# Last phase of a streaming encoder layer: transposes of u and y by the transfer engines, cached keys through two PSUM banks

## The chip, the cores and the metric

The kernel runs on one core of a Trainium2 chip. A core has five instruction streams that matter here: TensorE (PE, with its weight loads PEld), VectorE (DVE), ScalarE (ACT), GpSimd (POOL) and SyncE (SP); the last does nothing but issue transfers, which 16 DMA engines carry out. Every stream runs its instructions in the order in which they stand in it. The metric is the time of one execution in microseconds of device time. Before the change it is 2327.88 us, the median of three runs between 2325.01 and 2328.12.

## The reference

One layer of an encoder with two token mixers that work side by side, on a prompt of 2048 rows (16 tiles of 128) and on a "sample" batch of 8 sequences of 16 rows (one more tile of 128 rows), each sequence with 512 cached keys and values. Cut to what matters:

```
h, gate = adaln_modulate(x, c, norm_g, w_ada, b_ada)
qa, ka, va, za, qb, kb, vb, zb, ga, gb = project_inputs(h, w_in, pos)
oa = diff_attention(qa, ka, va, qpos, kpos, lam)          # 4 heads, two softmaxes each
ob = stick_breaking_attention(qb, kb, vb, qpos, kpos)     # 8 heads
oa = rms_norm(oa, subln_g) * (1.0 - lam_init)
ya = (oa.reshape(b, s, WIDTH_A) * silu(za)) @ w_branch_a  # 512 -> 1024
yb = (ob.reshape(b, s, WIDTH_B) * silu(zb)) @ w_branch_b  # 512 -> 1024
y  = sigmoid(ga) * ya + sigmoid(gb) * yb
x  = x + gate * (y @ w_out)                               # 1024 -> 1024
out = rms_norm(x, final_g)
```

For the sample rows the keys and values are the cached ones with the new ones behind them. The keys and values of all rows are outputs too.

## The kernel before

Up to about 1780 us of the profile the kernel projects h and runs the prompt's attention, one head (or pair of heads) after another, called a unit (8 units). z, the gates g, the attention's output o and, for the sample rows, q, k and v go to DRAM. The attention weights of the prompt are transposed there by transposing transfers (`turn`, line 568), which SP issues: for each, up to 128 rows by 2048 numbers of two bytes become 16 blocks of 128 x 128. These transfers are the one part of the kernel before that does with another tile what the change does with u and y.

The **last phase** (from line 1294 on, with its first tile begun earlier) goes through the 17 tiles of 128 rows, the sample tile as the last but one. For each tile:

- `inputs` (line 1162) loads o (line 1165) and z (line 1166), both into one buffer each (hs[0], hs[1]), and two halves of the gates (line 1170) into one of two pairs of buffers; it forms u = norm(o) * silu(z), and writes it as two float16 numbers, high and low part, into `u16` (hs[2], one buffer for all tiles).
- `turned` (line 1195) transposes u16, 16 blocks of 128 x 128: `transposed` (line 1155) sends 8 blocks through TensorE (line 1159) into one PSUM bank, and ScalarE copies the bank to SBUF (line 1160); twice. The destination has two buffers.
- `branches` (line 1201) multiplies u with the two branch weights: 48 matmuls of 512 columns (line 1210), four results of 12. VectorE and GpSimd apply the gates (lines 1212 and 1214), and `finish` splits the sum y into `y16`, high and low (lines 287 and 292), one buffer for all tiles.
- `turned_y` (line 1233) transposes y16 in the same way; here the destination has one buffer too, so the transpose of a tile's y waits until the products of the tile before have read theirs.
- `output` (line 1331) multiplies y with w_out: 48 matmuls of 512 columns (line 1344), two results of 24, then adds x, normalizes and stores (line 1358). The x of a tile is loaded at line 1337.

The sample attention runs beside the tiles. Eight units go through steps: four loads of keys (tile `dk`, line 716, two buffers) and four of values (`dv`, four buffers), 512 KB each; the transposes of the cached keys (line 735: two halves per load, four blocks each, into one PSUM bank `t` of which there is one, evicted to `dks` by VectorE for the first half and by ScalarE for the second, line 736); queries (line 721); scores (lines 745, 746, 752); weights (line 770, which waits for the softmax or the products on VectorE and GpSimd) and values (lines 784, 788).

In the source the work of step n is an interleaving, by written costs, of the branches of tile n, the output of tile n-1 and some steps of the sample units. The final order is set by a scheduler that plays the program through with its own costs of each instruction and lets each stream take what it takes to be ready; a change of one instruction's cost can therefore move many others. PSUM has eight banks: `mm` 2, `s` 3, `t` 1, `o` 2.

Of the kernel before, what the change touches and what calls it, by code (L numbers as in the profile page):

```python
# [17 lines left out]
F16 = mybir.dt.float16  # L18
# [7 lines left out]
P = 128  # L26
D = 1024
KT = D // P
# [82 lines left out]
def layer_kernel(ctx: ExitStack, tc: tile.TileContext, a: dict):  # L111
    nc = tc.nc
    V, S, G, T = nc.vector, nc.scalar, nc.gpsimd, nc.tensor
# [73 lines left out]
    def bank(tag, dt=F32):  # L187
        return ps.tile([P, 512 if dt == F32 else 1024], dt, tag=tag, name=f"ps_{tag}", bufs=BANKS[tag])
# [4 lines left out]
    id16 = con.tile([P, P], F16, name="id16")  # L193
# [507 lines left out]
    def sample(U, dec, fixed):  # L701
# [28 lines left out]
        def keys(i, half):  # L730
            if half == 0:
                box["k", i] = dec.tile([P, 8, P], F32, tag="dks", name="dks", bufs=4)
            pt = bank("t")
            for j in range(4):
                T.transpose(pt[:, j * P : (j + 1) * P], box[nk, i][:, half * 4 + j, :], ident)
            (S.copy if half else V.tensor_copy)(out=box["k", i][:, half * 4 : half * 4 + 4, :], in_=pt.rearrange("p (j n) -> p j n", n=P))
# [65 lines left out]
        for i in range(4):  # L802
            steps[2 + i] += [one(keys, i, 0), one(keys, i, 1)]
# [90 lines left out]
    with tc.tile_pool(name="p0", bufs=1) as p0:  # L894
# [25 lines left out]
        pt = bank("t")  # L920
# [231 lines left out]
        split(dst[:, 0, :, :], dst[:, 1, :, :], st, s, S if n % 2 else G)  # L1152
        return dst

    def transposed(x16, dst, half):

        pt = bank("s", F16)
        for k in range(KT):
            T.transpose(pt[:, k * P : (k + 1) * P], x16[:, half, k * P : (k + 1) * P], id16)  # L1159
        S.copy(out=dst[:, half * KT : (half + 1) * KT, :], in_=pt.rearrange("p (k n) -> p k n", n=P))  # L1160

    def inputs(t):

        o, z = hs[0:2]
        load(out=o, in_=o_d[t])
        load(out=z, in_=z_d[t])
        gs = []
        for j in range(2):
            gs.append(L["g"][(2 * len(begun) + j) % 4].rearrange("p (b n) -> p b n", b=2))
            load(out=gs[j], in_=g_d[t].rearrange("p (b n) -> p b n", b=2)[:, :, j * 512 : (j + 1) * 512])  # L1170
        begun.append(t)
        r = L["orms"][:, 4 * t : 4 * t + 4] if t < NT else rsqrt(osums[:, NT, :], 4, P, tiny, "rA")
        for n in range(2):
            c = slice(n * 512, (n + 1) * 512)
            sg = bank("mm")
            act(out=sg, in_=z[:, c], func=AF.Sigmoid)
            G.tensor_tensor(out=o[:, c], in0=o[:, c], in1=z[:, c], op=ALU.mult)
            if n == 1:
                V.tensor_tensor(out=o[:, c], in0=o[:, c], in1=sg, op=ALU.mult)  # L1179
            else:  # L1180
                for h in range(4):
                    c = slice(h * P, (h + 1) * P)
                    V.scalar_tensor_tensor(out=o[:, c], in0=sg[:, c], scalar=r[:, h : h + 1], in1=o[:, c], op0=ALU.mult, op1=ALU.mult)  # L1183
        for g in gs:
            act(out=g, in_=g, func=AF.Sigmoid)
        acc = tiny.tile([P, 1], F32, tag="uacc", name="uacc")
        sum_squares(o, D, acc)
        su = scales(acc, unit, "su")
        u16 = hs[2].bitcast(F16).rearrange("p (f n) -> p f n", f=2)
        split(u16[:, 0, :], u16[:, 1, :], o, su[:, 0:1], S)  # L1190
        iu = unit.tile([P, 1], F32, tag="iu", name="iu")
        V.tensor_tensor(out=iu, in0=su[:, 1:2], in1=L["s"][0][:, 1:2], op=ALU.mult)
        return dict(u16=u16, u=L["u"][len(begun) % 2], iu=iu, g=gs)

    def turned(st):

        st["u"] = st["u"].bitcast(F16).rearrange("p (k n) -> p k n", n=P)
        for half in range(2):
            transposed(st["u16"], st["u"], half)

    def branches(st):

# [29 lines left out]

    def turned_y(st):
        st["y"] = yT = L["y"].bitcast(F16).rearrange("p (k n) -> p k n", n=P)
        for half in range(2):
            transposed(st["y16"], yT, half)


    tiles = list(range(NT - 1)) + [NT, NT - 1]
# [15 lines left out]
    def early_work():  # L1255


        free.extend(units[7]["bufs"])

        def first(t):  # L1260
            if "orms" not in L:
                L["orms"] = rsqrt(osums[:, 0:NT, :].rearrange("p t h -> p (t h)"), 4 * NT, P, con, "orms")
            states[t] = inputs(t)
            if t == tiles[0]:
                turned(states[t])

        def early(i):

            if i == 0:
                L["first"] = [fn for _, fn in branches(states[tiles[0]])] + [lambda: turned_y(states[tiles[0]])]  # L1270
            L["first"][i]()

        def rest():
            L["g"], L["u"], (L["y"], L["y16"]) = free[0:4], free[4:6], free[6:8]

        return [branch_weight for _ in branch_weights] + [rest] + [lambda t=t: first(t) for t in tiles[0:2]] \
            + [lambda i=i: early(i) for i in range(5)]

    for n in range(first_step, len(steps) + PV_LAG):
        if n < len(steps):  # L1280
            u, t = steps[n]
# [23 lines left out]
    with ExitStack() as c2:  # L1305
# [8 lines left out]
        for j in range(2):  # L1314
            for k in range(0, KT, 2):
                st = s2.tile([P, D], F32, tag="x", name="x", bufs=2)
# [67 lines left out]
        for n in range(NT + 2):  # L1384
            work = []
            if 0 < n <= NT:
                work += branches(states[tiles[n]])
            if n + 1 <= NT:

                work.insert(2, (0.9, lambda n=n: turned(states[tiles[n + 1]])))  # L1390
            if n + 2 <= NT:
                work.insert(5, (0.1, lambda n=n: states.update({tiles[n + 2]: inputs(tiles[n + 2])})))
            if n > 0:
                work += output(tiles[n - 1], states.pop(tiles[n - 1]))
            if 0 < n <= NT:
                work.append((0.9, lambda n=n: turned_y(states[tiles[n]])))
            interleave(work, aside(n))
# [27 lines left out]
```

## Time and profile before

| | |
|---|---|
| median of three runs | 2327.88 us |
| the profiled execution: its own time | 2324.14 us |
| its span, first to last instruction | 2322.4 us |
| granted TensorE clock, mean | 0.971 |
| PE busy | 2115.7 us (91%) |
| DVE, ACT, POOL busy | 1615.7, 1545.4, 686.8 us |
| share of the 16 DMA engines of queue q1 | 67.0% |

The profile is of one execution. "Busy" adds up the time in which an engine has an instruction in work; TensorE's instructions overlap at their ends, so a short group of matmuls shows a few tenths of a microsecond more than its share of the stream. "Idle before" an instruction is the time for which its engine had nothing in work, with what ended it. A row of a timeline gives start, length, engine, line, operation, written tile <- read tiles, and the number of instructions merged into it. The DMA share is the mean busy share of 16 engines; packets overlap, so it can pass 1 for short times.

### The profile page before, as it was taken

The page shows a single profiled execution, that of the slowest core. Times are in us where ns is not written, and L with a number is a line of the kernel's source. Part 1 is how long each engine was busy: PE and PEld are TensorE (multiplying, and loading weights), DVE is VectorE, ACT ScalarE, POOL GpSimd, SP SyncE. Part 2 cuts the span into 40 slices and gives each one's busy share as a digit, 9 for nine tenths or more (in the row PEclk, how much of TensorE's full clock was granted, in tenths as well). Part 3 has the DMA queues.
Part 4 walks back from the last instruction along what each step waited for, and adds up shares of the span by engine and source line. Part 5 has one row for each costly group of instructions (what it writes and reads, how often), then busy time and mean ns, then how long its engine had stood idle before and what let it go on. Part 6 is the DMA issues. An engine that isn't in the chain of part 4 may idle for free. (4 is left out here: it accounts for less than half of the span.)

```text
span 2322.4 us, 41702 instructions
## 1 busy us (share of the span) xinstructions
PE 2115.7 (91%) x15022; PEld 1144.7 (49%) x15022; DVE 1615.7 (70%) x3523; ACT 1545.4 (67%) x3036; POOL 686.8 (30%) x575
## 2 busy tenths in 40 slices
PE   4997998998999999899999989999977889989898
PEld 2544554554555455455545545555544444545443
DVE  4677866789876678978667898776787545564654
ACT  3876767788766677876767787666776545465552
POOL 1522012255301235530123553022345222221222
PEclk8998999999999999999999999999978999999999
DMA  8559669697765679775576876667686766565521
GB/s 291 207 138 258 168 136 219 152 212 165 203 150 127 154 152 206 178 172 134 125 165 153 207 175 168 144 142 163 150 188 177 226 191 184 179 186 150 157 100 56
DMA packets 693840, 395.23 MB, mean 170 GB/s; under 512 B 454810, under 2 KB 638410, under 8 KB 693120
## 3 DMA queue, kind: packets, MB, share of 16 engines
q1 hardware_dynamic: 692554, 392.08, 67.0%
q8 instruction: 118, 1.93, 0.3%
q14 instruction: 90, 0.74, 0.1%
q10 hardware_dynamic: 1078, 0.48, 0.1%
HBM read 212.58 MB, written 72.91 MB: 123 GB/s over the span
## 5 line engine op out<-in xcount | busy, mean ns | idle before, releaser
L613 POOL TENSOR_TENSOR sc_p<-sc_p,sc_n 128x127 f32<-128x127 f32 (+7 forms) x192 | 308.3, 1610 | 782.1 <-DVE sc_n L607 761.7
L423 PE MATMUL ps_mm<-wb,hs 128*128 128x512 f16 x1632 | 412.2, 383 | 5.4 <-ACT gt L498 5.4
L423 PEld LDWEIGHTS <-hs 128*128 128x128 f16 x2976 | 263.1, 99 | 253.5 <-issue 21.2
L423 PE MATMUL ps_mm<-wa,hs 128*128 128x512 f16 x1344 | 337.0, 382 | 6.5 <-DVE v L292 4.7
L607 DVE TENSOR_TENSOR_SCAN sc_n<-ps_s,sc_n,zero_t 128x512 f32<-128x512 f32 x192 | 245.4, 1278 | 76.8 <-ACT ps_s L120 74.8
L120 ACT ACTIVATE sc_p<-ps_s,usc 128x512 f32<-128x512 f32 (+3 forms) x320 | 201.9, 631 | 99.7 <-PE ps_s L631 61.0
L630 PE MATMUL ps_s<-k,qst 128*128 128x512 f16 (+3 forms) x640 | 224.9, 352 | 42.6 <-DVE sc_n L607 31.7
L562 DVE TENSOR_TENSOR sc_n<-sc_p,sc_n 128x128 f16<-128x128 f32 (+7 forms) x192 | 211.6, 1108 | 44.3 <-ACT sc_n L561 44.1
L631 PE MATMUL ps_s<-k,qst 128*128 128x512 f16 (+3 forms) x640 | 224.9, 352 | 0.0
L682 PE MATMUL ps_o<-v,wt 128*128 128x128 f16 x1088 | 192.3, 225 | 28.3 <-DMA wt<-sc_n 28.2
L495 PE MATMUL ps_mm<-wa,hs 128*128 128x512 f16 x816 | 203.3, 379 | 1.2 <-DVE wa L292 1.2
L495 PE MATMUL ps_mm<-wb,hs 128*128 128x512 f16 x816 | 203.2, 379 | 0.0
L495 PEld LDWEIGHTS <-hs 128*128 128x128 f16 x1632 | 140.5, 98 | 123.3 <-issue 1.4
L561 ACT CAST sc_n<-sc_p 128x128 f16<-128x128 f32 (+7 forms) x192 | 153.0, 802 | 61.1 <-POOL sc_p L613 60.9
L120 ACT ACTIVATE ps_s<-ps_s,usc 128x512 f32<-128x512 f32 (+3 forms) x320 | 193.4, 604 | 0.0
L1344 PE MATMUL ps_o<-wo,wb 128*128 128x512 f16 x816 | 187.2, 382 | 0.7 <-ACT wb L1160 0.7
L683 PE MATMUL ps_o<-v,wt 128*128 128x64 f16 x1088 | 173.9, 198 | 0.0
L682 PEld LDWEIGHTS <-wt 128*128 128x128 f16 x1088 | 107.3, 101 | 107.5 <-DMA wt<-sc_n 35.4
L457 POOL TENSOR_TENSOR rot<-pr,rope 128x256 f32<-128x256 f32 x68 | 64.2, 944 | 272.7 <-ACT pr L437 224.7
L683 PEld LDWEIGHTS <-wt 128*128 128x128 f16 x1088 | 105.2, 100 | 72.2 <-issue 1.9
L607 DVE TENSOR_TENSOR_SCAN sc_n<-ps_s,zero_t 128x128 f32<-128x128 f32 (+3 forms) x128 | 104.6, 818 | 49.4 <-ACT ps_s L120 47.6
L1210 PE MATMUL ps_mm<-wa,wb 128*128 128x512 f16 x510 | 125.7, 385 | 3.1 <-DVE hs L1179 1.1
(327 smaller groups left out, 4290.8 us busy)
## 6 DMA issues: line engine op xcount, KB each, us to landing
hs<-hT_d SPq DMA_DIRECT2D x124, 512.0 KB, 4.2
g_d<-gt SPq DMA_DIRECT2D x68, 256.0 KB, 3.7
out_dram<-pr SPq DMA_DIRECT2D x204, 64.0 KB, 2.0
wide<-in_w_ada_dram SPq DMA_DIRECT2D x12, 1024.0 KB, 11.5
wa<-in_w_in_dram SPq DMA_DIRECT2D x36, 256.0 KB, 5.5
z_d<-pr SPq DMA_DIRECT2D x136, 64.0 KB, 1.7
o_d<-o SPq DMA_DIRECT2D x136, 64.0 KB, 2.5
hs<-z_d SPq DMA_DIRECT2D x17, 512.0 KB, 4.6
```

The source lines that it names most:

```text
L120: i = S.activation(**kw)
L423: T.matmul(box["p"], box["h"][:, hi, k, :], U["w"][k][:, wi, :], start=(n == 0), stop=(n == 3 * KT - 1))
L495: T.matmul(box["g"][:, 0:gw], box["h"][:, hi, k, :], U["wg"][k // per][:, k % per, wi, :], start=(j == 0), stop=(j == 3 * KT - 1))
L561: S.copy(out=hi, in_=src)
L562: V.tensor_tensor(out=lo, in0=src, in1=hi, op=ALU.subtract)
L607: V.tensor_tensor_scan(out=dst[:, lo : lo + n][:, ::-1], data0=src[:, 0:n][:, ::-1], data1=zero_t[:, 0:1].to_broadcast([P, n]), initial=fi ...
L613: G.tensor_tensor(out=p[:, 0:m], in0=p[:, 0:m], in1=n[:, 1 : m + 1], op=ALU.mult)
L630: T.matmul(p[:, 0:n], qst[:, c, :], kk[:, c, 0:n], start=True, stop=False)
L631: T.matmul(p[:, 0:n], qst[:, 2 + c, :], kk[:, c, 0:n], start=False, stop=not diag)
L682: T.matmul(po[:, c * P : (c + 1) * P], wt[:, wj, :], vt[:, c, :, :], start=first, stop=False)
L683: T.matmul(po[:, c * P : c * P + 64], wt[:, nb + wj, :], vt[:, c, 0, :], start=False, stop=last)
L1344: T.matmul(po, st["y"][:, yi * 8 + k, :], wo[j * 4 + k // 2][:, wi, k % 2, :], start=(n == 0), stop=(n == 3 * KT - 1))
```

## The change

Two edits, both in the last phase.

1. `turned` and `turned_y` no longer use TensorE and ScalarE. Each issues one transposing transfer on SP: 128 rows of 2048 float16 numbers become 16 blocks, u16 to the tile of u and y16 to the tile of y. The function `transposed` is gone, and with it per tile 32 transposes on TensorE, 4 copies on ScalarE and 4 uses of the PSUM banks `s`.
2. The two halves of a load of cached keys are transposed into different PSUM banks: the first half into `t` as before, the second into one of the three `s`.

```
@@ keys
-            pt = bank("t")
+            pt = bank("ts"[half])
             for j in range(4):
                 T.transpose(pt[:, j * P : (j + 1) * P], box[nk, i][:, half * 4 + j, :], ident)
             (S.copy if half else V.tensor_copy)(out=box["k", i][:, half * 4 : half * 4 + 4, :], in_=pt.rearrange("p (j n) -> p j n", n=P))
@@
-    def transposed(x16, dst, half):
-
-        pt = bank("s", F16)
-        for k in range(KT):
-            T.transpose(pt[:, k * P : (k + 1) * P], x16[:, half, k * P : (k + 1) * P], id16)
-        S.copy(out=dst[:, half * KT : (half + 1) * KT, :], in_=pt.rearrange("p (k n) -> p k n", n=P))
-
@@ turned
         st["u"] = st["u"].bitcast(F16).rearrange("p (k n) -> p k n", n=P)
-        for half in range(2):
-            transposed(st["u16"], st["u"], half)
+        nc.sync.dma_start_transpose(out=st["u"], in_=st["u16"].rearrange("p f n -> p (f n)"))
@@ turned_y
         st["y"] = yT = L["y"].bitcast(F16).rearrange("p (k n) -> p k n", n=P)
-        for half in range(2):
-            transposed(st["y16"], yT, half)
+        nc.sync.dma_start_transpose(out=yT, in_=st["y16"].rearrange("p f n -> p (f n)"))
```

Behind the edits line numbers fall by up to nine: 1210 becomes 1202, 1344 becomes 1335, 1170 becomes 1163, 1165 becomes 1158; the new transfers are lines 1191 (u) and 1227 (y). Up to the last two tiles of the prompt's attention the order of the instructions is the same; from there on the scheduler has made another one. Three places of it follow.

**TensorE, from the scores of a sample unit of the first mixer to its weights.** L752 are the last matmuls of the scores, L770 the transposes of the weights, which need the softmax done. L735 are key transposes of the next unit; L1159 the transposes of u (`hs_150`) and y that the change takes away; L1344 (now L1335) the output product and L1202 the branches. Matmuls and weight loads alternate; where rows repeat they are left out. Before:

```order
L752 MATMUL ps_s<-dks,qz 32x512 x16
L1159 LDWEIGHTS hs_150
...
L735 MATMUL ps_t<-ident,dk 128x128 x4
L1344 LDWEIGHTS wb_2006
...
L1159 LDWEIGHTS hs_150
...
L735 MATMUL ps_t<-ident,dk 128x128 x4
L770 MATMUL ps_s<-ident,dsc 128x128 x4
```

Now:

```order
L752 MATMUL ps_s<-dks,qz 32x512 x16
L1202 LDWEIGHTS wb_2005
...
L735 MATMUL ps_t<-ident,dk 128x128 x4
L735 MATMUL ps_s<-ident,dk 128x128 x4
L1335 LDWEIGHTS wb_2006
...
L735 MATMUL ps_t<-ident,dk 128x128 x4
L1335 LDWEIGHTS wb_2006
...
L735 MATMUL ps_s<-ident,dk 128x128 x4
L770 MATMUL ps_s<-ident,dsc 128x128 x4
```

Before, 4 matmuls of the output, 16 transposes of u and 8 of keys stand between scores and weights; now 28 matmuls of the branches, 24 of the output and 16 transposes of keys do.

**SP, late in the last phase, one tile's period.** g_d, o_d, z_d and x are the loads of gates, o, z and x for later tiles, out_dram is the store of a finished tile. Before:

```order
L1170 DMA wb_2008<-g_d_108 128x2x512
L1170 DMA wa_137<-g_d_108 128x2x512
...
L1166 DMA hs_149<-z_d_92 128x1024
L1165 DMA hs_148<-o_d_75 128x1024
L1358 DMA out_dram<-x_25221 128x1024
```

Now:

```order
L1163 DMA wb_2008<-g_d_108 128x2x512
L1163 DMA wa_137<-g_d_108 128x2x512
L1191 DMA_TRANSPOSE wb_2005<-hs_150 128x16x128
L1227 DMA_TRANSPOSE wb_2006<-wa_139 128x16x128
L1158 DMA hs_148<-o_d_75 128x1024
L1349 DMA out_dram<-x_24803 128x1024
```

Both transposes of a period stand between the loads of gates and the load of o, u of the tile two ahead first, y of the tile in work behind it.

**SP, at the start of the last phase.** wt is the transposed weight tile of the prompt's attention; dsam, dk and dv belong to the sample units; x<-in_w_out_dram are the loads of w_out. Now:

```order
L568 DMA_TRANSPOSE wt<-sc_n 128x16x128
L1191 DMA_TRANSPOSE wb_2010<-hs_150 128x16x128
L1158 DMA hs_148<-o_d_64 128x1024
L1151 DMA x<-in_w_out_dram 128x2x512 x2
...
L716 DMA dk<-in_cache_a_k_dram 128x8x128 x2
...
L716 DMA dv<-in_cache_a_v_dram 128x8x128
L1227 DMA_TRANSPOSE wb_2006<-wa_139 128x16x128
L1151 DMA x<-in_w_out_dram 128x2x512 x2
```

The transpose of the first tile's y stands behind four loads of w_out and the first loads of keys and values; before, TensorE did it while the prompt's attention ran out.

## The prediction

> **What bounds the kernel now.** I read the share of busy time by stretches first, since only the last phase is touched. Columns: length, busy time of each engine with its instructions, granted TensorE clock, DMA share, GB/s.
>
> ```profile
> core 0: us, PE busy (x) PEld busy (x) DVE busy (x) ACT busy (x) POOL busy (x), PEclk, DMA share, GB/s
> 1700.00:1780.00 80.00, 50.73 (x426) 32.80 (x425) 65.25 (x95) 60.32 (x96) 40.74 (x21) 0.72 0.73 153
> 1780.00:1850.00 70.00, 58.96 (x343) 29.78 (x342) 40.80 (x94) 37.48 (x56) 20.68 (x18) 0.93 0.84 265
> 1850.00:2200.00 350.00, 310.56 (x2481) 172.91 (x2480) 191.67 (x507) 181.90 (x323) 88.98 (x68) 0.96 0.58 176
> 2200.00:2290.00 90.00, 89.67 (x618) 45.13 (x616) 48.81 (x121) 39.99 (x61) 23.98 (x19) 1.00 0.25 88
> 2290.00:2322.40 32.40, 21.16 (x103) 9.16 (x101) 12.24 (x36) 7.44 (x12) 6.31 (x5) 0.90 0.10 39
> ```
>
> From 1780 to 2290 us TensorE has work for 459.2 of 510 us, and no other engine for much more than half. From 2200 on, where the sample units are done, it is never idle: what leaves its stream there shortens the program. Before 2200 it idles 11.0 + 39.4 = 50.4 us. The groups by line, from 1780 on, say where (last columns: idle before, and what ended it):
>
> ```profile
> L735 PE MATMUL ps_t<-ident,dk 128*128 128x128 f32 x256 | 41.7, 288 | 18.9 <-DVE dks L736 10.1 <-ACT wn L777 3.2 <-DMA dk<-in_cache_a_k_dram 2.5
> L770 PE MATMUL ps_s<-ident,dsc 128*128 128x128 f32 x48 | 9.1, 321 | 13.8 <-DVE dsc L594 10.9 <-POOL dsc L613 1.6 <-DVE dsc L607 1.3
> L745 PE MATMUL ps_s<-kn,qn 128*128 128x128 f32 x32 | 6.9, 326 | 7.3 <-DVE kn L728 7.3
> ```
>
> 40.0 of the 50.4 us belong to the sample units: key transposes that wait until their bank is evicted, weights that wait for the softmax, scores that wait for the queries' copy. So the phase is TensorE's stream plus stalls of that stream, both of which the change touches.
>
> **The transposes that leave TensorE.** The busy time of line 1159 counts overlapping ends; the price of one more transpose is the difference between a group of 16 and one of 8, (1.05 - 0.61) / 8 = 0.055 us.
>
> ```profile
> 1880.73 1.05 PE L1159 MATMUL ps_s<-id,wa 128*128 128x128 f16 x16 [0.53 <-DVE dsc L607]
> 1888.89 0.61 PE L1159 MATMUL ps_s<-id,hs 128*128 128x128 f16 x8
> ...
> 1780.00:1850.00 70.00, 4.17 (x55) 3.44 (x53) 0.93 0.84 265
> 1850.00:2200.00 350.00, 26.01 (x320) 22.92 (x320) 0.96 0.58 176
> 2200.00:2290.00 90.00, 7.81 (x112) 6.88 (x112) 1.00 0.25 88
> ```
>
> The three lower rows are line 1159 alone: 55 + 320 + 112 = 487 transposes, at 0.055 us **-26.8 us**, of which 6.2 after 2200, where nothing else hides them. The copies of line 1160 leave ScalarE, which has over half its time free: counted as nothing, even if they all stay uncovered for it.
>
> **The stalls.** With the second half in another bank, TensorE need no longer wait for VectorE's copy of the first. That ends most of the 10.1 us, and part of the 3.2 (the bank held by the weights' last copy). In the order of the change 52 matmuls of 512 columns stand between a unit's scores and weights where 4 stood; a matmul costs (8.15 - 5.79) / 11 = 0.215 us by the two groups below, so 11 us of work cover a wait of up to 4.3 us. Between queries and scores there are now mostly a dozen matmuls or more as well, but they were there in some units before too.
>
> ```profile
> 2289.27 8.15 PE L1344 MATMUL ps_o<-wo,wb 128*128 128x512 f16 x37
> 2294.94 0.75 DVE L292 SCALAR_TENSOR_TENSOR wa<-wa,sy,wa 128x512 f16<-128x512 f32 x1
> 2300.16 5.79 PE L1344 MATMUL ps_o<-wo,wb 128*128 128x512 f16 x26 [0.68 <-ACT wb L1160]
> ```
>
> Bounds: nothing (every stall finds another place) to all 40.0. I take 12 of 18.9, 11 of 13.8 and 3 of 7.3: **-26 us**.
>
> **What a transposing transfer costs.** The attention has 288 of them; a tile of u or y is as large as the largest.
>
> ```profile
> L568 SPq DMA_TRANSPOSE wt<-sc_n x280: 1175/1754/7207, 196.5 to 1776.2; - x140
> DMA to landing us min/median/max: 2.3/4.4/8.6
> ...
> 1757.40 8.91 SPq L568 DMA_TRANSPOSE wt<-sc_n  x3
> 1776.22 3.07 SPq L568 DMA_TRANSPOSE wt<-sc_n  x1
> ...
> 1765.90 0.23 PE L682 MATMUL ps_o<-v,wt 128*128 128x128 f16 x1 [1.90 <-DMA wt<-sc_n]
> 1768.98 0.29 PE L682 MATMUL ps_o<-v,wt 128*128 128x128 f16 x1 [2.03 <-DMA wt<-sc_n]
> 1781.58 0.23 PE L682 MATMUL ps_o<-v,wt 128*128 128x128 f16 x1 [1.10 <-DMA wt<-sc_n]
> ...
> 1758.00:1768.00 10.00, 7.04 (x57) 3.85 (x55) 9.93 (x15) 8.28 (x14) 5.33 (x3) 0.92 0.75 150
> 1784.00:1788.00 4.00, 4.00 (x26) 2.10 (x25) 1.95 (x2) 3.04 (x3) 0.08 (x1) 1.00 1.01 371
> ```
>
> The last one was issued at 1776.22 and its reader started at 1781.58: **5.4 us** from issue to use. Three in a row land 3.08 us apart and hold SP about 3 us each. From 1758 to 1768 they were alone and moved 1.5 MB, 2.86 transposes, in a DMA share of 7.5 us: **2.6 us of all 16 engines each**.
>
> [...]
>
> Between 1780 and 2200 stand 26 of the 33 added after the phase's begin, 26 x 2.6 = 68 us on top of 0.84 x 70 + 0.58 x 350 = 262. If the stretch shrinks to 385 us, the share is 330 / 385 = 0.86, as in 1780 to 1850, where TensorE lost 2.5 us to a late load of keys. Bounds 0 to +40 us (all stalls of the sample units come back as late loads); I take **+8**.
>
> Is the latency covered? In the order of the change at least 24 branch matmuls (5.2 us), in most tiles 36 and more (7.7 us), stand between the last output product of a tile, which frees the destination of y, and the first of the next. u is transposed two tiles ahead. Uncovered are the two ends. At the **end**, y of the last tile is ready at 2295.7 (the row of line 292 above), the 37 matmuls ended at about 2297.4, and the products began at 2300.16; now they begin 5.4 us behind the matmuls, at a clock that may have dropped by then (the stretch below, with gaps of 2 to 5 us in TensorE's stream, ran at half). +2.7 to +7; I take **+4**.
>
> ```profile
> 1766.00:1780.00 14.00, 6.72 (x76) 6.04 (x76) 12.83 (x21) 6.71 (x10) 8.08 (x5) 0.51 0.76 135
> ```
>
> At the **start**, the first y stands in SP's stream behind loads of values, which so far were issued at 1801.53; it lands at about 1808, whereas the first output product ran at 1790.60.
>
> ```profile
> 1801.53 0.43 SPq L716 DMA_DIRECT2D dv<-in_cache_a_v_dram  x1
> 1790.60 0.59 PE L1344 MATMUL ps_o<-wo,wb 128*128 128x512 f16 x2
> ```
>
> The next tile's 48 branch matmuls (10.3 us) and 16 key transposes cover most of these 17 us; what is behind it, the second sample step, waits as long. 0 to +12; I take **+6**. Before the phase, the first tile's branches (48 matmuls) now run among the last products of the attention, where TensorE idled, and VectorE reaches the attention's last weights earlier, but one transfer stands between theirs: -5 to +5, I take **-2**.
>
> **Sum.** -26.8 - 26 + 8 + 4 + 6 - 2 = -36.8 us. Against the profiled execution's own 2324.14 us (span 2322.4 plus 1.7 around it; 3.7 below the median of the runs, within their spread) that is 2287 us.
>
> **Rivals.**
>
> *More.* The transfers land in time and the stalls nearly vanish: all 40.0 us of them, +8 and +6 become 0, -26.8 - 40 + 4 - 2 = -65, with some left over about **2264**. For it speaks the spare room in the order; against it that the share of 0.86 is an average.
>
> *The DMA engines hold the stretch.* If they sustain 0.84 there, as in 1780 to 1850, and a transpose costs 3.07 us among other traffic, 1780 to 2200 takes (262 + 26 x 3.07) / 0.84 = 407 us instead of 420; with -6.2 behind it, +4 and -2: -17, **2307**.
>
> *Slower, by the same engines.* Above 3.6 us per transpose, (0.84 x 424 - 262) / 26, the stretch gets longer than everything else saves. At 4.5 it takes 451 us: +31 - 4 = **2351**. The longest issue of the row above, 7.2 us, shows that one can be held up; the median landing of 4.4 us, in stages whose share is not lower than here before the change, speaks against it (DMA share of the whole span in 40 slices, in tenths; the last phase is the last ten).
>
> ```profile
> DMA  8559669697765679775576876667686766565521
> ```
>
> *Slower, by exposure.* TensorE waits for each y, 16 times 5.4 us: +86 - 26.8 - 26 + 4 = +37, **2361**. It decides from the point at which SP issues y so late that 24 to 36 matmuls don't cover it, for instance behind a u that isn't ready. The order's distance speaks against it, and a tile's period of 350 / 9.9 = 35 us: the stretch holds 473 output matmuls (first row) and 480 of the branches, 96 a tile.
>
> ```profile
> 1850.00:2200.00 350.00, 107.51 (x473) 45.78 (x472) 0.96 0.58 176
> 1850.00:2200.00 350.00, 113.32 (x480) 47.30 (x480) 0.96 0.58 176
> ```
>
> [...]
>
> *No change.* The saved time turns into other waits of the same stream: **2324**.
>
> **How the numbers follow.** Forecast 0.58, more 0.13, DMA-bound 0.14, slower by the engines 0.07, by exposure 0.04, no change 0.04. About 0.2% (4.7 us) is what a measurement of this kernel can tell from nothing. Faster: 0.58 + 0.13 + 0.13 = 0.84, where 0.01 of the DMA-bound case is left for a stretch that saves nothing; within: 0.04 + 0.01 = 0.05; slower 0.07 + 0.04 = 0.11. The range from 2262 (nearly all stalls gone) to 2314 (the DMA-bound case with a late end) leaves out the last three cases and little else.
>
> **What would show it.** TensorE's busy time from 1780 on lower by some 27 us; no idle over a microsecond at L770 and little at L735; the share from 1780 to 2200 near 0.85, transposes landing within 5 to 6 us; the last output product some 5.4 us behind the one before. Wrong it would be if output products (line 1335) wait for the transfer of line 1227 tile by tile, if key loads come late throughout, or if SP holds loads back behind a transpose that waits for its source.

## The result, and the profile after

The change makes the kernel 1.1% faster: 2298.0 us (median of four runs, 2295.6 to 2302.0) against 2326.5 us of the kernel before in the same session (2325.0 to 2328.1); ratio 0.9888, 95% interval 0.9874 to 0.9903. A second measurement on another chip gave 0.9876 (0.9855 to 0.9898). The forecast was 2287; the gain is some 28 us instead of 37.

The share of busy time by stretches, first the kernel before, now over the whole last phase (columns as above):

```profile
1780.00:2322.40 542.40, 480.36 (x3539) 256.98 (x3537) 293.51 (x756) 266.80 (x451) 139.95 (x110) 0.96 0.53 164
```

The changed kernel, the same view:

```profile
1780.00:2300.10 520.10, 449.47 (x3020) 224.80 (x3019) 289.39 (x768) 211.16 (x391) 145.32 (x112) 0.95 0.76 202
```

The phase is 22.3 us shorter; the medians differ by 28.5, since the profiled execution of the kernel before lies 2.4 us below its median and that of the change 4.0 above. TensorE's busy time fell by 30.9 us, but its idle time (length less busy) rose from 62.0 to 70.6. The DMA engines' load grew from 0.53 x 542.4 = 287 to 0.76 x 520.1 = 395 us of all 16 engines, for 32 transposing transfers: 3.4 us each.

The groups by line of the changed kernel, from 1780 on, answer to the three rows of the prediction:

```profile
L1335 PE MATMUL ps_o<-wo,wb 128*128 128x512 f16 x816 | 199.6, 400 | 30.3 <-DMA wb<-wa 25.5 <-POOL wo L289 2.5 <-DVE wa L1204 1.8
L735 PE MATMUL ps_t<-ident,dk 128*128 128x128 f32 x128 | 20.5, 282 | 7.7 <-DVE dks L736 6.3 <-DVE col L281 0.8 <-ACT gate L1373 0.7
L735 PE MATMUL ps_s<-ident,dk 128*128 128x128 f32 x128 | 19.5, 274 | 4.9 <-DVE dsc L607 4.9
L770 PE MATMUL ps_s<-ident,dsc 128*128 128x128 f32 x48 | 7.0, 275 | 1.9 <-POOL dsc L613 1.9
L745 PE MATMUL ps_s<-kn,qn 128*128 128x128 f32 x32 | 5.7, 288 | 0.0
L776 PE MATMUL ps_t<-ident,dsc 128*128 128x128 f32 x12 | 3.6, 299 | 10.5 <-DVE dks L736 10.4
```

The 40.0 us of stalls at L735, L770 and L745 are 14.5 now. In their place stand two that the kernel before did not have: 25.5 us in which the output products wait for y's transfer, and 10.4 us at L776.

**What a wait costs beside its length.** The 816 output products take longer too: 199.6 us busy in the row above, 187.2 in the kernel before:

```profile
L1344 PE MATMUL ps_o<-wo,wb 128*128 128x512 f16 x816 | 187.2, 382 | 0.7 <-ACT wb L1160 0.7
```

Behind the waits of 3.3 to 6.8 us for y the granted clock (third figure from the end) was 0.50 to 0.61. Here are the four microseconds behind the wait of 4.42 us that is shown next, and a stretch soon after:

```profile
1912.38:1916.38 4.00, 4.00 (x12) 1.58 (x13) 0.00 (x0) 0.00 (x0) 0.94 (x1) 0.61 0.87 270
1916.00:1920.00 4.00, 4.00 (x23) 2.09 (x21) 2.47 (x7) 0.60 (x1) 1.93 (x2) 1.00 0.72 230
```

Behind the two stalls at L776 (5.16 and 5.24 us) the clock was 0.57 and 0.50 for as long, behind the waits of 1.5 to 2.5 us for y 1.00. The kernel before has this too (0.50 behind a wait of 4.27 us at L770). So a wait with such a clock behind it costs, by an estimate from these figures, some 1.6 to 2 us (4 us at 0.61 to 0.50) more than the idle time shows, and the busy time holds a part of the price of the waits.

**Where the waits for y come from.** SP's timeline, and TensorE's, around one of the eight:

```profile
1899.41 1.88 SPq L716 DMA_DIRECT2D dv<-in_cache_a_v_dram  x2
1901.38 4.94 SPq L1191 DMA_TRANSPOSE wb<-hs  x1
1906.41 3.97 SPq L1227 DMA_TRANSPOSE wb<-wa  x1
```

```profile
1895.70 1.03 PE L1335 MATMUL ps_o<-wo,wb 128*128 128x512 f16 x4
...
1907.37 0.60 PE L735 MATMUL ps_s<-ident,dk 128*128 128x128 f32 x4
1912.38 1.46 PE L1335 MATMUL ps_o<-wo,wb 128*128 128x512 f16 x3 [4.42 <-DMA wb<-wa]
```

The products that free y's destination ended at 1896.7. SP was at loads of values and a store, then issued u for 4.94 us, and y only at 1906.41, 9.7 us late. TensorE did 36 branch matmuls and the scores meanwhile, and had nothing left by 1908.

**Where the 10.4 us at L776 come from.** Here o is late. SP, GpSimd, ScalarE, VectorE and TensorE of the changed kernel, for one of the two stalls:

```profile
1994.89 5.99 SPq L1227 DMA_TRANSPOSE wb<-wa  x1
2000.93 0.58 SPq L716 DMA_DIRECT2D dv<-in_cache_a_v_dram  x1
2001.56 0.57 SPq L1158 DMA_DIRECT2D hs<-o_d  x1
...
2007.24 2.50 POOL L1170 TENSOR_TENSOR hs<-hs,hs 128x512 f32<-128x512 f32 x2 [12.52 <-issue]
...
2010.99 0.63 ACT L274 ACTIVATE junk<-wa 128x512 f16<-128x512 f32 x1 [7.62 <-POOL wa L1206]
...
2013.72 1.13 DVE L1176 SCALAR_TENSOR_TENSOR hs<-ps_mm,orms,hs 128x128 f32<-128x128 f32 x4 [8.51 <-ACT ps_mm L120]
...
2016.91 0.68 DVE L736 COPY dks<-ps_t 128x512 f32<-128x512 f32 x1
...
2017.64 0.33 PE L776 MATMUL ps_t<-ident,dsc 128*128 128x128 f32 x1 [5.16 <-DVE dks L736]
```

The load of o stood behind y's transfer and was issued at 2001.56. GpSimd's first product of the new u began at 2007.24 (the profile names no releaser; that it waited for o is read from the times), ScalarE waited for GpSimd until 2010.99, VectorE's next step of u stood in its queue until 2013.72, and behind it the copy of keys that TensorE's bank t waited for. But for y's transfer, none of these instructions was touched by the change.

### The profile page after: what moved, and what is told of

The parts are those of the page before. It is cut to its first block, busy times and chain, and to the rows that moved or that the text cites. A ratio compares the mean times of both kernels' runs of the same rounds, so it can differ in the third digit from the quotient of the medians.

```text
span 2300.1 us, 40624 instructions
## 1 busy us (share of the span) xinstructions
PE 2088.9 (91%) x14478; PEld 1111.0 (48%) x14478; DVE 1609.4 (70%) x3523; ACT 1482.1 (64%) x2968; POOL 688.5 (30%) x575
## 5 line engine op out<-in xcount | busy, mean ns | idle before, releaser
L1335 PE MATMUL ps_o<-wo,wb 128*128 128x512 f16 x816 | 199.6, 400 | 30.3 <-DMA wb<-wa 25.5
L682 PE MATMUL ps_o<-v,wt 128*128 128x128 f16 x1088 | 192.5, 225 | 26.2 <-DMA wt<-sc_n 26.0
L1335 PEld LDWEIGHTS <-wb 128*128 128x128 f16 x816 | 81.9, 102 | 135.4 <-DMA wb<-wa 31.1
```

What stands on the lines that cost most here:

```text
L682: T.matmul(po[:, c * P : (c + 1) * P], wt[:, wj, :], vt[:, c, :, :], start=first, stop=False)
L1335: T.matmul(po, st["y"][:, yi * 8 + k, :], wo[j * 4 + k // 2][:, wi, k % 2, :], start=(n == 0), stop=(n == 3 * KT - 1))
```

## The experiments

All kernels were timed against the kernel before on the same chip. "Idle" is the length from 1780 us to the end of the profiled execution, less TensorE's busy time there. The profiled execution is one of the runs and lies up to 4.8 us from its median; in the profiles the attention's last product ends between 1773 and 1785 us, so the stretch doesn't hold quite the same work each time. Two profiles of the change differ by 1.1 us in busy and 2.0 in idle time. A difference of a few microseconds in these two columns says nothing.

| kernel | median us | before | ratio (95%) | TensorE busy | idle |
|---|---|---|---|---|---|
| before | | | | 480.4 | 62.0 |
| the change, first session | 2298.0 | 2326.5 | 0.9888 (0.9874 to 0.9903) | 449.5 | 70.6 |
| the change, again (f1_full) | 2297.1 | 2325.1 | 0.9876 (0.9855 to 0.9898) | 448.3 | 68.6 |
| keys' bank alone (e1_banks) | 2302.4 | 2329.2 | 0.9886 (0.9867 to 0.9906) | 476.1 | 48.7 |
| transfers alone (e2_transfers) | 2316.7 | 2329.2 | 0.9949 (0.9931 to 0.9966) | 456.5 | 74.7 |
| bank, u by transfer (e3_u_only) | 2302.8 | 2329.2 | 0.9899 (0.9881 to 0.9916) | 463.4 | 57.4 |
| bank, y by transfer (e4_y_only) | 2292.4 | 2329.2 | 0.9846 (0.9829 to 0.9863) | 456.1 | 53.4 |
| as e4, last y on TensorE (f2_y_last) | 2291.2 | 2325.1 | 0.9850 (0.9832 to 0.9869) | 457.1 | 57.2 |
| y ahead of u (g3_y_first) | 2290.0 | 2325.1 | 0.9845 (0.9829 to 0.9861) | 446.8 | 61.2 |
| plain transfers, u and y left untransposed (g4_plain) | 2282.0 | 2325.1 | 0.9795 (0.9775 to 0.9815) | 443.8 | 60.6 |
| o loaded by GpSimd (h3_o_on_pool) | 2328.4 | 2325.9 | 1.0006 (0.9987 to 1.0025) | 450.3 | 91.7 |
| y ahead, in halves (h1_first_halves) | 2282.0 | 2325.9 | 0.9811 (0.9792 to 0.9830) | 448.1 | 56.3 |
| as e4, y in halves (h2_y_only_halves) | 2294.9 | 2325.9 | 0.9867 (0.9848 to 0.9885) | 457.7 | 53.0 |
| as h1, queries in a bank s (i1_queries) | 2281.4 | 2323.8 | 0.9815 (0.9801 to 0.9828) | 439.3 | 57.6 |

**Theory A** after the two traces: the stream is shorter by the transposes, and the stalls that the bank and the new order removed came back as waits made by the transfers. Then the two edits should add, less what the transfers cost. Rivals: **B**, the bank is the whole gain; **C**, the stalls follow the order, whatever the edit; **D**, the DMA engines set the length of the stretch.

### The parts alone

```
e1_banks, e2_transfers (against the kernel before)
e1:  -            pt = bank("t")
     +            pt = bank("ts"[half])
e2:  -            transposed(st["u16"], st["u"], half)   and the same for y16
     +        nc.sync.dma_start_transpose(out=st["u"], in_=st["u16"]...)   and the same for y16
```

> Only the second bank for the keys is taken over; u and y stay on TensorE and ScalarE. Theory A (two halves that add: TensorE's stream loses 27 us of transposes, and what the sample units stalled, 36 us, comes back as 25.5 us of waits for y and 10.4 us of waits behind a late VectorE copy, both made by the transfers): here the stream keeps its 487 transposes, and the stalls go without the transfers to bring them back. All of the 40 us at L735, L770 and L745 less what the order leaves: 8 to 25 us gained, 2302 to 2318; no wait at L1335 over 1 us, L770 under 3. Rival B (the second bank is the whole gain): 2298, as the full change. Rival C (the stalls follow the order, and the bank has no part): 2324 to 2327, L735 still near 19 and L770 near 14.

> Only u and y go by transposing transfers; the keys keep one bank. Theory A: TensorE's stream is 27 us shorter, the stalls at L735 and L770 (33 us) largely stay, and the waits for y come on top of them, but waits overlap: y has longer to land where TensorE stalls elsewhere. 2300 to 2315. Rival B (the bank is the whole gain): 2324 or more, slower if the 25.5 us of waits for y come in full. Rival D (the DMA engines set the stretch, so that neither TensorE's stream nor its stalls matter): 2298, as the full change, with the same share of 0.84 to 0.87 from 1780 to 2180.

Measured: the bank alone gives 0.9886, as much as the whole change; the transfers alone give 0.9949. Theory A's range held for the bank at its very edge (2302.4) and was missed by 2 us for the transfers (2316.7); B is wrong that the transfers give nothing by themselves, and D that they give all. What fell is that the parts add. Alone they save 26.7 and 12.4 us, together 28.5. Rival C's time fell (it had 2324 to 2327), but its mechanism did not. Each kernel has an order of its own, made by the scheduler. In the three units whose weights waited over 3 us for the softmax at L770, 0 to 4 matmuls of 512 columns stood between scores and weights; with the bank alone 56 stand there. L770 waited there for VectorE's softmax and for no bank, so that its fall from 13.8 us to the 1.9 of the row below points to the order. How much of the 26.7 us is the bank and how much the order that came with it stays open: no run has the one without the other. The waits of TensorE with the bank alone (us in total, times, longest):

```profile
PE ps_s L735 <- DVE dsc L607: 8.0, 2, 5.8
PE ps_t L721 <- DVE dks L736: 4.9, 3, 2.1
...
PE ps_s L770 <- DVE dsc L607: 1.9, 1, 1.9
```

With the transfers alone:

```profile
PE ps_o L1342 <- DMA wb<-wa: 26.5, 9, 7.1
PE ps_s L745 <- DVE kn L728: 17.0, 5, 7.5
PE ps_s L770 <- POOL dsc L613: 4.5, 1, 4.5
PE ps_t L735 <- DVE dks L736: 3.9, 6, 0.8
```

The waits for y are as long without the bank (26.5) as with it (25.5); they belong to the transfers. With one bank as before, the wait for VectorE's copy at L735 is 3.9 us here instead of 10.1, and L770 waits 4.5 instead of 13.8: 23 to 27 output products stand between scores and weights of the same three units. So these stalls go without the second bank too, while L745 waits 17.0 instead of 7.3. The 10.4 us at L776 are in neither kernel: they come up only where both edits meet.

### u alone and y alone

```
e3_u_only, e4_y_only (against the change)
e3:  turned_y   -  nc.sync.dma_start_transpose(out=yT, ...)
                +  for half in range(2): transposed(st["y16"], yT, half)
e4:  turned     -  nc.sync.dma_start_transpose(out=st["u"], ...)
                +  for half in range(2): transposed(st["u16"], st["u"], half)
```

> The full change with y put back on TensorE and ScalarE; u by transfer. Theory A: the 25.5 us of waits at L1335 vanish, 256 or so transposes at 0.055 us (14 us) come back, the half of the added DMA load goes (16 transfers at 3.3 us, share from 0.87 to about 0.75), and so do the 10.4 us at L776 and the 4 us of the tail: 2275 to 2290, faster than the full change. Rival D (the DMA engines set the stretch): the load falls by 16 x 3.3 = 53 us, so about the same or faster too, but then with TensorE still idle over 40 us from 1780 on. Rival C (the waits are the order's and only change their name): 2298 to 2312, the stalls back at L735 and L770.

> The full change with u put back on TensorE and ScalarE; y by transfer. Theory A: y no longer stands behind a u in SP's queue and meets half the added load: the waits at L1335 fall from 25.5 us to 5 to 15, 14 us of transposes come back on TensorE, the tail stays: 2293 to 2306. Rival D (the load alone counts): as with u only, 2275 to 2290.

Measured: 2302.8 with u alone, 2292.4 with y alone. Theory A had it the other way round, and D had 2275 to 2290 for y alone. u alone lies in C's range, but without the stalls at L735 and L770 that C expected back (11.6 and 2.1 us, as with the bank alone). With the bank in place, u's transfer brings nothing (0.9899 against 0.9886), y's brings 10 us, and both together are no better than the bank alone. TensorE's busy time falls each time: against the bank alone by 12.7 us with u, 20.0 with y, 26.6 with both. That 12.7 and 20.0 don't add to 26.6 shows how rough such a difference is. The idle time grows by 8.7, 4.7 and 21.9 us. The last is clear; the difference between u and y is not, and why y alone is 10 us faster than u alone is shown only in part. TensorE's waits with u alone:

```profile
PE ps_t L721 <- DVE dks L736: 9.3, 5, 2.6
...
PE ps_t L776 <- DVE dks L736: 4.0, 3, 2.5
```

Nobody waits for u itself: it is two tiles ahead. What grows are waits behind VectorE's copies of keys (13.3 us at L721 and L776 against 4.9). And with y alone:

```profile
PE ps_o L1343 <- DMA wb<-wa: 10.2, 5, 3.3
```

Without u on SP the waits for y are 10.2 us instead of 25.5. That suggests SP's queue (theory **Q**: a transposing issue holds SP for several us, 1.7 to 7.4 for y in the change, and what stands behind it is late) against the load of the engines (**L**).

### The queue or the load

```
g3_y_first (against the change): u's transfer waits for the product that frees y's destination
     turned   +        if "m" in L:
              +            G.tensor_copy(out=st["u"][0:1, 0, 0:1], in_=L["m"][0:1, 0:1])
     output   +                L["m"] = m
g4_plain (against the change)
     turned   -        nc.sync.dma_start_transpose(out=st["u"], ...)
              +        nc.sync.dma_start(out=st["u"], in_=st["u16"]...)      and the same for y
```

> The change as it is, beside the others of this group: 0.9888 of the time before, as in the first measurement. With u left on TensorE it was 0.9846; this run says on one chip whether u's transfer costs 8 to 10 us more than it saves.

> The full change, with one tiny GpSimd copy that makes u's transfer wait for the output product that frees y's destination, so that SP issues y ahead of u in every tile; TensorE's order and the DMA load stay the same. Theory Q (SP's queue: u's issue of 3 to 7 us holds up y): the waits for y fall from 25.5 us to about the 10 us that they are with y alone: 2280 to 2288, ratio 0.981 to 0.985. Theory L (the load of the DMA engines makes y late, in whatever order): 2295 to 2300, with waits over 20 us. Against both: if u comes late now, TensorE waits for u (L1204) and the time is 2298 or more.

> The full change with the two transposing transfers replaced by plain ones of the same bytes from and to the same tiles; u and y are not transposed, so the output is another one, and the time is that of the rest. Theory A (the transposing transfers are dear: 3.3 us of all engines and 2 to 7 us of SP each): the added load falls from 109 to about 33 x 1.4 = 46 us, SP is free after a microsecond, the waits for y fall below 5 us and those at L776 vanish: 2255 to 2272, near the 2264 of the rival that has nearly all stalls gone. Rival (any transfer of 512 KB at this place comes too late, since its latency counts): 2288 to 2298.

Measured: y ahead of u is 2290.0, where the change itself is 2297.1 on this chip: 7 us, with TensorE's order largely the same and the engines' share from 1780 to 2180 the same (0.85). That is 2 us above Q's range, with the ratio inside it, and clearly below L's: the load alone is not the cause, and rival D, by which the engines set the stretch, fell for this share. But theory Q had named the wrong waits, and those for y stayed above 20 us, as L had it. TensorE's waits with y ahead:

```profile
PE ps_o L1337 <- DMA wb<-wa: 21.6, 9, 6.4
PE ps_t L721 <- DVE dks L736: 6.7, 4, 3.9
```

The waits for y fell by 4.6 us only (26.2 in f1_full). What went away are the 10.6 us at L776: in this order SP issues the load of o first, then y, then u.

Plain transfers of the same bytes give 2282.0, 15 us better. This kernel leaves out the transposing of u and y, so its output is not the layer's and only its time counts. The 15 us are the price of transposing in the engines and on SP, and of whatever the order does, which the scheduler made anew here. The share of the 16 engines by queue from 1780 on, of the change and of the plain transfers:

```profile
DMA packets 154226, 104.37 MB, mean 202 GB/s; under 512 B 69432, under 2 KB 137016, under 8 KB 154188
...
q1 hardware_dynamic: 154188, 103.87, 75.6%
```

```profile
DMA packets 92428, 104.44 MB, mean 207 GB/s; under 512 B 3403, under 2 KB 71115, under 8 KB 92390
...
q1 hardware_dynamic: 92390, 103.94, 64.6%
```

For the same bytes 75.6% of 517 us against 64.6% of 504: (391 - 326) / 32 = 2.0 us of all engines more per transposing transfer, and 66,000 packets of less than 512 bytes more. The 1.4 us that theory A counted for a plain one are 524 KB at the 371 GB/s of the plain loads from 1784 to 1788 in the kernel before; here it took (0.65 x 504.4 - 287) / 32 = 1.3 us. Theory A had expected more of the plain transfers, 2255 to 2272, because the waits for y should have gone too, and its rival less, 2288 to 2298; the time lies between. The waits did not go. Line 1227 with plain transfers, its issues, who waited for it, and its landing:

```profile
L1227 SPq DMA_DIRECT2D wb<-wa x17: 471/500/2638, 1793.4 to 2257.8; - x17
...
  PE ps_o L1335: 21.7, 8
...
DMA to landing us min/median/max: 2.9/5.0/9.1
```

SP is free after 0.5 us (median), and still y lands 5.0 us after its issue and TensorE waits for it 21.7 us. y is issued late here too: before one of the eight waits its destination was free at 1979.2, and SP came to y at 1986.7, behind the issues of a store and three loads, 0.4 to 2.7 us each. The change's own line 1227:

```profile
L1227 SPq DMA_TRANSPOSE wb<-wa x17: 1722/3574/7413, 1795.0 to 2271.3; - x17
...
DMA to landing us min/median/max: 4.3/4.8/9.4
```

The transposing transfer landed after 4.8 us. So most of the waits for y are not the price of transposing. Sent among the loads of keys and values, y's 512 KB came about 5 us after their issue either way.

### The last y

```
f2_y_last (against e4_y_only), in turned_y
     +        if st.get("last"):
     +            for half in range(2): transposed(st["y16"], yT, half)
     +        else:  (the transfer)
```

> Keys in two banks and y by transfer, u on TensorE, and the y of the last tile on TensorE as before. The gap before the last 24 products was 4.4 us plus matmuls at a lower clock with the transfer, 2.7 us without: 3 to 5 us below y alone, 2287 to 2289 or 0.983. If the end does not follow the last tile's y: 2292, 0.9846.

Measured: 0.9850, the same as y alone within the intervals. Around the place itself 3.0 us are saved (from the end of the products before to the end of the last ones 14.4 us instead of 17.4), which this measurement cannot tell from nothing in the total.

### The load of o, and y in halves

```
h3_o_on_pool (against the change):      -  load(out=o, in_=o_d[t])      +  nc.gpsimd.dma_start(out=o, in_=o_d[t])
h1_first_halves (against g3_y_first), h2_y_only_halves (against e4_y_only), in turned_y
     -  nc.sync.dma_start_transpose(out=yT, in_=st["y16"]...)
     +  for half in range(2):
     +      nc.sync.dma_start_transpose(out=yT[:, half * KT : (half + 1) * KT, :], in_=st["y16"][:, half, :])
```

> The full change with the load of o (L1158) issued by GpSimd instead of SP, so that it no longer stands behind a transposing transfer; all else as in the change, and from the sixth tile on TensorE's order too. Theory Q (SP held by the transposes makes o late, o makes u's first steps late, VectorE's queue then holds the eviction of the keys: the two waits of 5.2 us at L776): those 10.4 us vanish, the waits for y stay near 25: 2286 to 2291, ratio 0.983 to 0.986, as with y first. Rival (the order y before u alone made the difference there): 2295 to 2300 with 10 us at L776.

> y ahead of u on SP, and y by two transfers of 8 blocks, the high part first: the first 16 of 24 products need only that. Theory X (what is left of the waits for y, 21.6 us, is the time that any transfer takes to land here, 4 to 7 us): the high part lands 1.5 to 2.5 us earlier in each of eight tiles, so the waits fall to 8 to 14 us: 2277 to 2284. Rival (the first half queues behind the same loads of keys and gains nothing, while SP issues 17 transfers more): 2288 to 2294.

> Keys in two banks, u on TensorE, y by two transfers of 8 blocks, the high part first. Waits for y are 10 us with one transfer: theory X has 3 to 6 us less, 2286 to 2289, ratio 0.982 to 0.983; the rival has 2291 to 2294.

**o by GpSimd** is a clear miss: 2328.4 (2311 to 2335), no faster than the kernel before. The waits at L776 are gone as theory Q said, but TensorE now waits for y 47.1 us:

```profile
PE ps_o L1335 <- DMA wb<-wa: 47.1, 9, 9.0
```

The stretch from 1850 to 2180 and the queues of this kernel say why the run is no test of Q's time:

```profile
1850.00:2180.00 330.00, 275.78 (x2085) 145.29 (x2084) 173.82 (x479) 136.13 (x263) 90.45 (x74) 0.93 0.95 214
```

```profile
q1 hardware_dynamic: 152551, 96.31, 77.9%
q0 software_dynamic: 2016, 7.34, 6.9%
...
hs<-o_d POOLq DMA_DIRECT2D x14, 512.0 KB, 10.5
```

The DMA share is 0.95 there, where the change has 0.83 at 215 GB/s (f1_full). The 14 loads on the second queue take 6.9% of 520 us = 36 us, 2.6 us each, and the first queue takes more for fewer bytes (77.9% of 520 = 405 us for 96 MB, against 391 us for 104 MB in the change). This resembles the forecast's rival "slower by the same engines", reached by another way. That the engines hold the stretch at a share of 0.95 is argued, not shown: SP's issues of y grew as well (median 5.1 us, 3.6 in the change), and GpSimd waited 88.9 us for o. Why the first queue's packets took more time here stays open.

**y in halves, ahead of u** gives 2282.0, the fastest with i1. The time is theory X's; the waits for y are gone more thoroughly than it said, which the products allow: the last 8 of a tile read only the low part, so the high part's place is free 8 products earlier, and the first 16 of the next need nothing else. TensorE's waits:

```profile
PE ps_t L721 <- DVE dks L736: 10.5, 4, 4.5
PE ps_s L735 <- DVE dsc L607: 7.5, 3, 5.1
...
PE ps_o L1338 <- DMA wb<-wa: 1.5, 3, 0.7
```

21.6 us of waits became 1.5, and the time fell by 8 us (ratio 0.9845 to 0.9811); the idle time fell by 5, since L721 and others took up the rest. **With u on TensorE** the same halves brought nothing (0.9867 against 0.9846, in different sessions): there 10.2 us of waits for y went and the idle time stayed (53.4 and 53.0). On one chip, u by transfer behind y (2282.0) is now 13 us faster than u on TensorE (2294.9), give or take 6 by the two intervals. That fits what the 240 transposes of u from 1780 on cost at 0.055 us: 13 us. Between the two profiled executions TensorE's busy time falls by 9.6. So where u's transfer is out of the way of y, its gain arrives, as closely as this can be told.

### Does a stall go with its bank?

```
i1_queries (against h1_first_halves), in queries
     -            pt = bank("t")
     +            pt = bank("s")
```

> y ahead of u, y in two halves, and the transposes of the queries (L721) in one of the s banks instead of bank t, so that they no longer wait until VectorE has copied the keys out of bank t. With y first in halves, 10.5 us of waits stood at L721 behind VectorE's copy (L736), in four places of up to 4.5 us. If a stall that is named by one bank goes with that bank: 2272 to 2277, ratio 0.977 to 0.979. If stalls of VectorE's late queue only move to the next instruction that needs it (L745, L735 or L770): 2279 to 2285, ratio 0.980 to 0.982, with TensorE idle for about 56 us from 1780 on as without it.

Measured: 0.9815, the same as without. The 10.5 us at L721 are gone, and 10 us more stand at L735, where a bank s now waits for VectorE's scan (line 607) of the stick-breaking weights:

```profile
PE ps_s L735 <- DVE dsc L607: 17.8, 3, 7.4
```

The idle time is 57.6 us, as before the edit (56.3). What TensorE waits for there is VectorE's queue; for this stall the bank only decides at which instruction.

## Why the prediction was right, and where it was off

The sign, the range (2262 to 2314) and the two causes were right; the middle was 11 us too low. By its own steps:

- **The transposes, -26.8.** Right in size; a closer agreement would be luck. TensorE's busy time falls by 476.1 - 449.5 = 26.6 us between the bank alone and the change, by 30.9 between the kernel before and the change, and by 23.9 between the kernel before and the transfers alone. Each is a net figure: it holds the 12 us and more by which the output products grew (187.2 us before, 186.9 with the bank alone, 199.6 in the change, 201.5 with the transfers alone), for which no step had a term.
- **The stalls, -26.** Right for the lines that it named: 40.0 to 14.5 us, and the bank alone measured -26.7. L770 and L745 went as far as they could (1.9 and 0), L735 kept 12.6. The two reasons given, bank and order, are not separated by any run; with one bank and a new order L735 and L770 wait less as well.
- **The start, +6.** Right in size: y was issued at 1795.0 and its first product began at 1804.45 (forecast 1808) after 6.8 us of idling; the granted clock was 0.50 in the 4 us behind it.
- **The end, +4.** Right: from the end of the products before to the end of the last ones 14.4 us in the kernel before, 18.5 now, with 3.3 us of waiting for the last y.
- **The contention, +8.** This is the step that failed. The transposes cost 3.4 us of all engines each, not 2.6; and the loss was sought in late loads of keys, which did not come (no wait for dk in the change's list). It came as 25.5 - 6.8 - 3.3 = 15.4 us of waits for y in the middle of the phase and 10.4 us at L776: 26 us where 8 stood, and behind those of 3.4 to 5.2 us among them TensorE's granted clock was 0.50 to 0.61 for 4 us, which the idle time doesn't hold.
- **"Uncovered are the two ends."** Here is the reason. The cover of 24 to 36 branch matmuls was held against 5.4 us from issue to use, as if SP issued y the moment the destination came free. In the trace SP was 1.3 to 9.7 us late with it from the third tile to the thirteenth, mostly with u's issue of 3 to 7 us in front. The rival "by exposure" had this mechanism ("behind a u that isn't ready"), but u was ready: its issue alone held the queue. Its price of 5.4 us for every tile was too high, since eight waited and for 3.2 us on average.
- **What no step had:** the load of o behind a transposing transfer, and from there by GpSimd, ScalarE and VectorE to a bank of TensorE. The order of SP that stands ahead of the prediction shows o's place behind both transposes, but only y's and u's were costed.
- **The sum.** Alone each part was sized well: -26 for the bank (measured -26.7), -26.8 + 8 + 4 + 6 - 2 = -10.8 for the transfers (measured -12.4). Their sum was not: 28.5 measured. That the two edits draw on the same slack, the work that TensorE has in hand while something else is late, is argued; no run tests it. What the runs show is that the loss lay in how u and y were sent: with y ahead of u and in halves both edits together save 43.8 us, more than the 39.1 of the parts.
- **The rival "the DMA engines hold the stretch"** (2307) was nearer to the measured time than its chance of 0.14 suggests, yet not by its mechanism: at a share of 0.85 from 1780 to 2180 y ahead of u is 7 us faster, and at 0.86 y in halves 15 us.

What would have shown it: the list at the end of the prediction named the waits of line 1335 for line 1227 as what would prove it wrong, and they were there in half of the tiles.

## What to carry to other kernels

Price a transfer that replaces work of an engine by three things: the time of the DMA engines (3.4 us each here), the time for which its issue holds the queue (1.7 to 7.4 us for y), and everything that stands behind it in that queue, whoever needs it (the load of o, with 10.4 us at L776). Here the order in the queue was worth 7 us of 2297, and transposing transfers against plain ones, with the order that came with each, 15. Count the cover of a just-in-time transfer from its issue in the queue, not from the moment its source is ready, and send what is needed first in a piece of its own: y ahead of u and in two halves took the change from 0.988 to 0.981. Two edits that each remove waits of one stream need not add: measure them alone and together, and look at the idle time and not at the name of the wait, since a removed wait can stand at the next instruction that needs the same late engine (10.5 us at L721 became 10 at L735 in i1_queries).

## What the runs showed of the hardware that was not expected

- A transposing transfer of 512 KB took about 3.4 us of all 16 engines in this traffic, 2.0 more than a plain one of the same tiles, in some 2,000 small packets each; y's issue held SP for 1.7 to 7.4 us (median 3.6) where a plain one held it for 0.5 to 2.6 (median 0.5).
- From issue to landing y took 4.8 us by a transposing transfer and 5.0 by a plain one, u 7.5 (f1_full) and 6.6 (medians).
- Loading o from GpSimd's queue instead of SP's took 2.6 us of all engines for each 512 KB and 10.5 us to land (4.3 from SP in f1_full, medians), and the share of the stretch from 1850 to 2180 was 0.95 at 214 GB/s where f1_full has 0.83 at 215; that kernel was 31 us slower than the change.
- Behind a wait of 3.3 to 6.8 us of the output products for y, the granted TensorE clock was 0.50 to 0.61 for the next 4 us; behind waits of 1.5 to 2.5 us it was 1.00 (all in the profile of the change). No threshold follows: in the same profile it was 0.63 behind a wait of 2.51 us for wo and 1.00 behind one of 2.84 us at L735.
